# Gate and up products by Strassen's seven products, in a hybrid decoder layer on one core

## The chip, the core and the metric

The kernel runs on one core of a Trainium2 chip. The metric is the device time of one execution in microseconds (us): the median of several runs. One execution was also recorded by the hardware profiler, and every row below is of that execution.

## The reference, cut to what matters

One decoder layer is applied to 1,088 tokens: a prompt of 1,024 and 8 x 8 sample tokens, 1,024 features wide, in 32-bit floats. In order:

- x += 0.5 * (silu(h W_gate) * (h W_up)) W_down, with h = RMSNorm(x); W_gate and W_up are 1,024 x 2,816, W_down is 2,816 x 1,024 (FFN a);
- h = RMSNorm(x), multiplied by w_in (1,024 x 4,096): queries, keys, values, the input u of a state space model (SSM) and two gates; sliding-window attention; the SSM with its own tables of coefficients, followed by a gated linear unit (GLU); the gated sum of both branches times w_out is added to x;
- a second FFN of the same form with weights of its own (FFN b), then a last RMSNorm.

The outputs are y, the key and value windows and the SSM states.

## The kernel before

**Numbers.** Each 32-bit operand of a large product is split in two parts that TensorE multiplies fast: hi, a copy rounded by ScalarE, and lo, the difference from VectorE or GpSimd (`split`, L98). A product then is three: hi·hi, hi·lo, lo·hi (`mm3`, L102). The tokens are on the columns, in three chunks of 384, 384 and 320 (`CH`, L15). x lies in SBUF as 8 tiles of 128 features x 1,088 tokens.

**FFN.** `gu_unit` (L333) makes one tile of 128 of the 2,816 hidden features: per chunk 24 gate products, silu, 24 up products, their product, and its split, which stays in SBUF. `d_unit` (L404) multiplies two or three such tiles by their rows of W_down and adds to x, with VectorE reading PSUM (L432). `ffn_units` (L1467) puts two `gu_unit` before each `d_unit`, so hidden tiles live shortly. The last `d_unit` of FFN a is followed by the next norm, chunk by chunk (`norm_steps`, L291); FFN b ends in `last_unit`, which also makes the output.

**The order of work** is the order in which the program is written out, since the scheduler is in manual mode: every engine and every DMA queue executes its own instructions in that order. `run_units` (L1439) calls for each unit `load` two units ahead (DMAs on SP's queue), `prep` one unit ahead (the splits), and `main`. At each `yield` of a `main`, `tick` (L1420) issues one or more steps of `pending` (norm steps) and, at the rate given, steps of one side job: during FFN a that is `ssm_setup` (L512), started at the first `d_unit` at 0.55 steps per tick. It has 193 steps: the first issues the loads of the parameters, the second transposes `lam` on TensorE, then come small steps with two `pow` on GpSimd (L565, L574), and from step 25 on eight blocks of 21 steps (L673 to L762) that build the tables, almost all of it on VectorE.

**The beginning.** `start_first` (L177) loads three tiles of x, transposes them, and lets the first products of gate and up run on x without the factor of the norm, which is multiplied in afterwards.

**After the mixer**, x is written to DRAM (L936) and reloaded before w_out (`x_reload`, L1386); `wo_unit` (L1391) adds to x and prepares the norm of FFN b.

Of the kernel before, what the change touches and what calls it, by code (L numbers as in the profile page):

```python
# [12 lines left out]
D = 1024  # L13
KC = 8
CH = ((0, 384), (384, 384), (768, 320))  # L15
# [11 lines left out]
# sin x = x (1 + z p(z)), cos x = 1 + z q(z), z = x^2, |x| <= pi/2  # L27
# [4 lines left out]
# columns of the constants: identity, half-swap, block index, sign, parity masks | attention masks, selection  # L32
# [30 lines left out]
class Kern:  # L63
    def __init__(s, ctx, tc, a, o):
# [6 lines left out]
        E(tc.manual_schedule())  # L71
        s.pending = []
# [29 lines left out]
    def mm3(s, ps, ops, every=8):  # L102
        n = 3 * len(ops)
        i = 0
        for wh, wl, xh, xl in ops:
            for w, x in ((wh, xh), (wh, xl), (wl, xh)):
                s.nc.tensor.matmul(ps, w, x, start=i == 0, stop=i == n - 1)  # L107
                i += 1
                if i % every == 0 and i < n:
                    yield  # L110
# [15 lines left out]
    def consts(s):  # L126
# [13 lines left out]
        s.mhalf = s.cst.tile([128, 3], F32, name="mhalf")  # L140
# [3 lines left out]
        s.x = [s.B([128, T], f"x{k}", F32) for k in range(KC)]  # L144

    def htiles(s, ph):
        s.hh = [s.B([128, T], f"hh{k}_{ph}") for k in range(KC)]
        s.hl = [s.B([128, T], f"hl{k}_{ph}") for k in range(KC)]

# [1 line left out]
    def rstd_of(s, c, ms, ph):  # L151
        r = s.small([128, 3], "rstd", 2)
        s.nc.gpsimd.tensor_tensor(r, ms, s.mhalf, op=OP.pow)  # L153
        return r
# [7 lines left out]
    def h_of(s, c, k, rbc, g, eng=None):  # L162
        o, n = CH[c]
        t = s.t(f"hraw{g}_{c}_{k}")
# [3 lines left out]
    def load_x(s, c):  # L168
        nc = s.nc
        for i in range(3 * c, 3 * c + 3):  # L170
# [4 lines left out]
            s.xt.append((t, m))  # L175

    def start_first(s, prep):  # L177
        """the first chunk: h without the factor of the norm, which the first products take instead"""
        nc = s.nc
        V, A = nc.vector, nc.scalar  # L180
        n = CH[0][1]
        g = s.gains[:, 0]
        ssq = s.small([128, 2, 3], "ssq", 2)
        ps = [s.bank(t, f"xtr0_{k}") for k, t in enumerate("aabbmddd")]

        def stats(i):
            t, _ = s.xt[i]
            j1, j2 = s.sm([128, 512], f"junk0_{i}"), s.sm([128, 512], f"junka0_{i}")
            V.scalar_tensor_tensor(j1, t[:, 0:512], 1.0, t[:, 0:512], op0=OP.mult, op1=OP.mult, accum_out=ssq[:, 0, i:i + 1])
            A.activation(j2, t[:, 512:1024], AF.Square, accum_out=ssq[:, 1, i:i + 1])  # L190

        def xc(k):
            if k % 2:
                V.tensor_copy(s.x[k][:, :n], ps[k][:, :n])
            else:
                A.activation(s.x[k][:, :n], ps[k][:, :n], AF.Copy)

        def h(k):
            A.activation(s.hh[k][:, :n], s.x[k][:, :n], AF.Copy, scale=g[:, k:k + 1])
            V.scalar_tensor_tensor(s.hl[k][:, :n], s.x[k][:, :n], g[:, k:k + 1], s.hh[k][:, :n].bitcast(F32), op0=OP.mult, op1=OP.subtract)  # L200

        for i in range(3):
            for k in range(KC):
                nc.tensor.transpose(ps[k][:, i * 128:(i + 1) * 128], s.xt[i][0][:, k * 128:(k + 1) * 128], s.id)
        for i in range(3):
            stats(i)
        ms = s.small([128, 3], "ms", 2)
        V.tensor_add(ms, ssq[:, 0, :], ssq[:, 1, :])
        V.tensor_scalar(ms, ms, 1.0 / D, 1e-6, op0=OP.mult, op1=OP.add)
        rs = s.rstd_of(0, ms, "s")  # L210
        for k in range(0, KC, 2):
            xc(k)
            xc(k + 1)
            h(k)
            if k == 0:
                next(prep)
            h(k + 1)
        next(prep)
        s.hready = 1

        def spread():
            rb = s.spread(0, rs, "s")
            s.rbc0 = s.sm([128, n], "rbc0")
            A.activation(s.rbc0, rb[:, :n], AF.Copy)
        return [spread], [lambda: next(prep)] * 2

    def start_steps(s, c):
        nc = s.nc
        V, A = nc.vector, nc.scalar
        o, n = CH[c]  # L230
        st = {}

        def stats(i, m):
            if "ssq" not in st:
                st["ssq"] = s.small([128, 2, 3], "ssq", 2)
                if n < 384:
                    V.memset(st["ssq"], 0.5)
            t, _ = s.xt[3 * c + i]
            x, y = t[:m, 0:512], t[:m, 512:1024]
            j1, j2 = s.sm([128, 512], f"junk{c}_{i}"), s.sm([128, 512], f"junka{c}_{i}")  # L240
            A.activation(j2[:m], y, AF.Square, accum_out=st["ssq"][:m, 1, i:i + 1])
            V.scalar_tensor_tensor(j1[:m], x, 1.0, x, op0=OP.mult, op1=OP.mult, accum_out=st["ssq"][:m, 0, i:i + 1])

        def rstd():
            ms = s.small([128, 3], "ms", 2)
            V.tensor_add(ms, st["ssq"][:, 0, :], st["ssq"][:, 1, :])
# [1362 lines left out]
```

## Time and profile before

| | |
|---|---|
| median of 3 runs | 2387.35 us (2383.14 to 2388.43) |
| span of the profiled execution, first to last instruction | 2384.7 us |
| TensorE (PE) products, busy | 2349.1 us, 99% of the span |
| VectorE (DVE) busy | 1123.1 us, 47% |
| ScalarE (ACT) busy | 687.7 us, 29% |
| GpSimd (POOL) busy | 169.2 us, 7% |
| DMA | 182.88 MB, 77 GB/s over the span |

No time is given for the profiled execution beyond its span; the span lies 2.65 us under the median of the runs. In the rows, PEld is TensorE's loading of weights, which overlaps its products, and SP is the engine that issues most DMAs. A name such as psga is the PSUM tile of the gate product in FFN a, psdb that of the down product in FFN b. A product's busy time includes its latency; its cost in a stream is the distance from one start to the next.

### The profile page before, as it was taken

What the parts mean: (1) busy time and instruction counts of PE and PEld (TensorE: products, weight loads), DVE (VectorE), ACT (ScalarE), POOL (GpSimd) and SP (SyncE); (2) the same over time, 40 slices, a digit from 0 to 9 for tenths busy, and PEclk for the clock granted to TensorE, in tenths of its full rate; (3) what the DMA queues carried; (4) which work ended last, traced back from release to release, by engine and by line L of the source; (5) the groups of instructions that cost most, each with busy time, mean ns of one, the idle gap of its engine ahead of it and who ended that gap; (6) DMA issues with size and microseconds to landing.
All of it is one profiled execution on the core that took longest, in us unless ns stands there. A gap on an engine that the chain in (4) does not pass through costs nothing. (4 is left out here: it accounts for less than half of the span.)

```text
span 2384.7 us, 34882 instructions
## 1 busy us (share of the span) xinstructions
PE 2349.1 (99%) x14361; PEld 2296.1 (96%) x14361; DVE 1123.1 (47%) x2362; ACT 687.7 (29%) x1483; POOL 169.2 (7%) x241
## 2 busy tenths in 40 slices
PE   8999999999999999999999999999999999999998
PEld 7999999999999997999998999999999999999997
DVE  5655455554432622447773766353332333332324
ACT  5212221222111341246665642231111111111123
POOL 3400000000000130002120200040000000000000
PEclk9999999999999999999999999999999999999999
DMA  5212222222301137631234264101111111111102
GB/s 150 63 47 64 80 63 63 80 64 78 111 27 54 37 144 221 214 93 36 60 83 108 74 227 151 52 27 45 40 50 51 39 53 37 48 41 45 50 22 75
DMA packets 249615, 182.88 MB, mean 77 GB/s; under 512 B 47120, under 2 KB 231504, under 8 KB 249424
## 3 DMA queue, kind: packets, MB, share of 16 engines
q1 hardware_dynamic: 247664, 178.34, 25.4%
q8 instruction: 113, 1.85, 0.3%
q10 hardware_dynamic: 1376, 2.29, 0.3%
q14 instruction: 46, 0.38, 0.0%
q0 software_dynamic: 416, 0.02, 0.0%
HBM read 143.50 MB, written 41.17 MB: 77 GB/s over the span
## 5 line engine op out<-in xcount | busy, mean ns | idle before, releaser
L365 DVE TENSOR_TENSOR sgb<-sgb,psub 128x384 f32<-128x384 f32 (+1 forms) x66 | 35.1, 532 | 270.6 <-PE psub L107 262.7
L432 DVE SCALAR_TENSOR_TENSOR x<-psda,x 128x384 f32<-128x384 f32 (+1 forms) x240 | 125.8, 532 | 68.1 <-PE psda L107 67.5
L432 DVE SCALAR_TENSOR_TENSOR xr<-psdb,xr 128x384 f32<-128x384 f32 (+1 forms) x216 | 114.6, 534 | 83.3 <-PE psdb L107 82.7
L359 ACT ACTIVATE sgb<-psgb 128x384 f32<-128x384 f32 (+1 forms) x66 | 31.3, 474 | 388.2 <-PE psgb L107 388.2
L365 DVE TENSOR_TENSOR sga<-sga,psua 128x384 f32<-128x384 f32 (+1 forms) x66 | 35.0, 530 | 183.9 <-PE psua L107 183.4
L359 ACT ACTIVATE sga<-psga 128x384 f32<-128x384 f32 (+1 forms) x64 | 30.2, 472 | 241.0 <-PE psga L107 241.0
L99 ACT ACTIVATE hidhb<-sgb 128x384 fp32r<-128x384 f32 (+1 forms) x66 | 33.5, 507 | 225.3 <-DVE sgb L365 225.3
L99 ACT ACTIVATE hidha<-sga 128x384 fp32r<-128x384 f32 (+1 forms) x66 | 33.5, 507 | 210.5 <-DVE sga L365 210.5
L1151 POOL TENSOR_SCALAR sm<-sm,sum 128x256 f32<-128x256 f32 x128 | 60.2, 492 | 311.7 <-DVE sum L1149 195.8
L100 POOL TENSOR_TENSOR hl_a<-hraw,hh_a 128x384 fp32r<-128x384 f32 (+1 forms) x72 | 74.5, 1066 | 46.9 <-ACT hh_a L99 42.4
L153 POOL TENSOR_TENSOR rstd<-ms,mhalf 128x3 f32<-128x3 f32 x9 | 8.0, 885 | 927.7 <-DVE ms L304 903.8
L1135 ACT ACTIVATE sm<-sm,nm 128x256 f32<-128x256 f32 x128 | 63.3, 503 | 2.0 <-DVE nm L1122 1.9
L498 POOL TENSOR_TENSOR rf<-msf,mhalf 128x1 f32<-128x1 f32 (+1 forms) x9 | 4.9, 543 | 773.0 <-DVE msf L497 773.0
L100 DVE TENSOR_TENSOR hidla<-sga,hidha 128x384 fp32r<-128x384 f32 (+1 forms) x66 | 35.9, 544 | 38.2 <-ACT hidha L99 38.2
L100 DVE TENSOR_TENSOR hidlb<-sgb,hidhb 128x384 fp32r<-128x384 f32 (+1 forms) x66 | 35.6, 539 | 38.4 <-ACT hidhb L99 38.4
L1118 DVE CUSTOM_DVE_ANT_0 sm<-S,c 128x256 f32<-128x256 f32 x128 | 46.2, 417 | 5.6 <-PE S L1115 5.4
L99 ACT ACTIVATE hh_a<-hraw 128x384 fp32r<-128x384 f32 (+1 forms) x72 | 35.5, 507 | 28.1 <-DVE hraw L165 26.7
L1182 DVE TENSOR_TENSOR ptl<-PT,pth 128x512 fp32r<-128x512 f32 x60 | 38.8, 686 | 3.8 <-ACT pth L1181 3.0
L1204 DVE TENSOR_TENSOR Os<-Os,O 64x256 f32<-64x256 f32 x64 | 26.7, 418 | 26.1 <-ACT Os L1201 25.5
L1181 ACT ACTIVATE pth<-PT 128x512 fp32r<-128x512 f32 x60 | 32.8, 596 | 20.9 <-PE PT L1179 20.6
L1179 PE MATMUL PT<-c,sm 128*128 128x128 f32 x240 | 34.2, 276 | 2.2 <-POOL sm L1151 0.8
L1179 PEld LDWEIGHTS PT<-c,sm 128*128 128x128 f32 x240 | 28.2, 140 | 6.3 <-POOL sm L1151 5.3
(1792 smaller groups left out, 8281.0 us busy)
## 6 DMA issues: line engine op xcount, KB each, us to landing
rgatea<-in_ffn_a_gate_dram SPq DMA_DIRECT2D x22, 512.0 KB, 3.9
rupa<-in_ffn_a_up_dram SPq DMA_DIRECT2D x22, 512.0 KB, 5.2
rdowna<-in_ffn_a_down_dram SPq DMA_DIRECT2D x22, 512.0 KB, 4.5
rgateb<-in_ffn_b_gate_dram SPq DMA_DIRECT2D x22, 512.0 KB, 3.7
rupb<-in_ffn_b_up_dram SPq DMA_DIRECT2D x22, 512.0 KB, 3.9
rdownb<-in_ffn_b_down_dram SPq DMA_DIRECT2D x22, 512.0 KB, 3.5
tab<-tab SPq DMA_DIRECT2D x20, 384.0 KB, 5.9
tab<-tab SPq DMA_DIRECT2D x10, 480.0 KB, 4.9
```

The lines of the kernel that those rows point to most:

```text
L99: s.nc.scalar.activation(hi, raw, AF.Copy)
L100: (eng or s.nc.vector).tensor_sub(lo, raw, hi.bitcast(F32))
L359: nc.scalar.activation(sg[:, :n], pg[:, :n], AF.Silu)
L365: nc.vector.tensor_mul(sg[:, :n], sg[:, :n], pu[:, :n])
L432: nc.vector.scalar_tensor_tensor(xs, ps[:, :n], 0.5, xs, op0=OP.mult, op1=OP.add)
L1118: V.tensor_tensor_reduce(out=sm[:, h, :], in0=ps[:, par * 256:(par + 1) * 256], in1=mask, scale=0.125, scalar=-1e30, op0=OP.add, op1=OP.ma ...
L1135: A.activation(sm[:, h, :], sm[:, h, :], AF.Exp, bias=nm[:, h:h + 1], accum_out=sm4[:, h:h + 1])
L1151: s.nc.gpsimd.tensor_scalar(sm[:, h, :], sm[:, h, :], sm4[:, h:h + 1], 1.0, op0=OP.mult, op1=OP.mult)
L1179: TE.transpose(ps[:, c:c + 128], sm[:, h, kb * 128:(kb + 1) * 128], s.id)
L1181: A.activation(hi, ps, AF.Copy)
L1182: V.tensor_sub(lo, ps, hi.bitcast(F32))
L1204: V.tensor_add(o[r, 0:256], o[r, 0:256], ps[r, c])
```

## The change

- **Gate and up** are seen as one 2 x 2 block product (two halves of the 1,024 input features; gate and up as the two rows) and two groups of tokens as the columns, and are computed by the seven products of Strassen's scheme in place of eight. For this the 1,088 tokens are cut in four quarters of 272: each half of the tokens (`sub`) is a pair of quarters (`e`). Seven operands per half are made from h and split (`hop_steps`: b11, t1 to t4, b21, b22), and seven per tile from the weights (a11, a12, a22, s1 to s4), with four sums on GpSimd (`sums`), seven hi parts on ScalarE and seven lo parts on VectorE, three steps ahead of their use. A unit of the stage is a tile with both halves of the tokens; the first two and the last two tiles are done one half at a time, which makes 26 units. Each product is 12 matmuls of 272 columns. Where Strassen adds products, they accumulate in one PSUM bank across products (X, V).
- The hidden tiles go to DRAM unsplit (`hd`), one DMA per tile and half on SP's queue.
- **Down is a stage of its own** after all of gate and up: eight `d_unit` of 2, 3, 3, 3, 3, 3, 2 and 3 hidden tiles, which load W_down and the hidden tiles and split both; in FFN a the lo parts are made on GpSimd, in FFN b on VectorE. x is written to DRAM before the stage and reloaded in it, four tiles ahead (`need_x`).
- `ssm_setup` still starts with the first `d_unit`, so it now runs in the down stage of FFN a alone, at 1.6 steps per tick.
- The first half of the tokens is normed and all its seven operands are made before the first product (`start`); the second half is made in steps beside the first two units. Before FFN b the same is done in the last `wo_unit` (`normed`).
- GLU and w_out use the four chunks of 272 as well.

The core of the diff:

```diff
-CH = ((0, 384), (384, 384), (768, 320))
+QC = 272
+HC = 2 * QC
+
+CH = {0: (0, 384), 1: (384, 384), 2: (768, 320), 10: (0, QC), 11: (QC, QC), 12: (2 * QC, QC), 13: (3 * QC, QC)}
+CP, CQ = (0, 1, 2), (10, 11, 12, 13)
...
+    def hop_steps(s, sub, R):
+
+        V, P = s.nc.vector, s.nc.gpsimd
+        t = {}
+
+        def sum(n, a, b, into, eng):
+            def f():
+                x = s.B([128, 4, QC], f"{n}raw{sub}", F32) if into is None else R[into]
+                eng.tensor_sub(x, get(a), get(b))
+                t[n] = x
+            return f
+
+        def get(k):
+            return t[k] if k in t else R[k]
+
+        def h(n, k, eng=V):
+            return lambda: s.hsplit(sub, n, get(k), eng)
+        return [h("b11", (0, 0)), sum("t1", (1, 0), (0, 0), None, V), sum("t2", (1, 1), "t1", None, V), h("t2", "t2"), h("t1", "t1"),
+                sum("t3", (1, 1), (1, 0), (1, 0), P), h("b21", (0, 1)), h("t3", "t3"), sum("t4", (0, 1), "t2", (0, 1), P),
+                h("b22", (1, 1)), h("t4", "t4")]
...
+    def normed(s, c):
+
+        sub, e = divmod(c - 10, 2)
+        o = CH[c][0]
+        if e == 0:
+            s.R = s.quarters(sub)
+        R = s.R
+
+        def raw(k, rbc):
+            s.nc.vector.scalar_tensor_tensor(R[e, k // 4][:, k % 4, :], s.x[k][:, o:o + QC], s.gains[:, 2, k:k + 1], rbc[:, :QC], op0=OP.mult, op1=OP.mult)
+        s.pending += s.norm_steps(c, "o", 2, raw)
+        if e:
+            if sub:
+                def spill():
+                    s.x_spill()
+                    s.x = {}
+                s.pending.append(spill)
+            s.pending += s.hop_steps(sub, R)
...
+        for i in range(5):
+            load(i)
+        g.load()
+        for i in range(5, 9):
+            load(i)
+        nc.sync.dma_start(s.c1[:, C_SW:], s.a["c1"][:, C_SW:])
...
+        R = s.quarters(0)
+        for k in range(KC):
+            raw(0, R, k)
+        st = s.hop_steps(0, R)
+        for f in st:
+            f()
+            next(prep, None)
+        for _ in prep:
+            pass
+        for q in range(4):
+            spill(0, q)
...
+        units = [[(j, h)] for h in range(2) for j in range(2)] + [[(j, 0), (j, 1)] for j in range(2, NFF - 2)]
+        units += [[(j, h)] for h in range(2) for j in range(NFF - 2, NFF)]
+        N = len(units)
+        raw, ops, st, hid = {}, {}, {}, {}
+        LEAD = 3
+        steps = []
+        for n in range(N):
+            steps += [("P1", n)] + ([("D", n - 1)] if n else []) + [(k, n) for k in ("P6", "P5", "P27")]
+        steps.append(("D", N - 1))
+        made = {"P1": ("a11",), "D": ("a22", "s4"), "P6": ("s2",), "P5": ("s1",), "P27": ("s3", "a12")}
...
+            g, u = raw[n][:2]
+            if kind == "P6":
+                s1 = s.sm([128, 4, 128], f"s1{ph}{n}")
+                P.tensor_add(s1, u[:, 0:4], u[:, 4:8])
+                P.tensor_sub(u[:, 0:4], g[:, 0:4], u[:, 0:4])
+                P.tensor_sub(g[:, 0:4], s1, g[:, 0:4])
+                raw[n] = g, u, s1
+            if kind == "D":
+                P.tensor_sub(g[:, 4:8], g[:, 4:8], g[:, 0:4])
...
+                    def hi(name=name, n=n2):
+                        w = s.B([128, 2, 4, 128], f"{name}{ph}{n}")
+                        A.activation(w[:, 0], source(name, n), AF.Copy)
+                        ops[n, name] = w
+
+                    def lo(name=name, n=n2):
+                        w = ops[n, name]
+                        V.tensor_sub(w[:, 1], source(name, n), w[:, 0].bitcast(F32))
+                    out += [hi, lo]
+            if i + 1 < len(steps):
+                kind, n = steps[i + 1]
+                if kind in ("P6", "D"):
+                    out.append(lambda: sums(kind, n))
...
+        def prod(ps, n, a, sub, b, more):
+            w = ops[n, a]
+            bh, bl = s.need_op(sub, b)
+            yield from s.mm3(ps[:, :QC], [(w[:, 0, k, :], w[:, 1, k, :], bh[:, k, :], bl[:, k, :]) for k in range(4)], 6, more)
...
+        def p6(n, e):
+            j, sub = units[n][e]
+            d = st[n, e]
+            yield from prod(d["X"], n, "s2", sub, "t2", True)
+            d["u"] = s.t(f"u{ph}{j}_{sub}")[:, :QC]
+            A.activation(d["u"], d["X"][:, :QC], AF.Copy)
...
+        def p3(n, e):
+            j, sub = units[n][e]
+            d = st[n, e]
+            yield from prod(d["V"], n, "s4", sub, "b22", True)
+            V.tensor_add(d["u"], d["u"], d["V"][:, :QC])
+            A.activation(d["u"], d["u"], AF.Silu)
+            P.tensor_mul(d["h2"], d["h2"], d["u"])
+            o = sub * HC
+            nc.sync.dma_start(s.hd[j, :, o:o + HC], hid[j][:, o:o + HC])
...
+                    r = s.B([128, T], f"rhid{ph}{j}", F32)
+                    nc.sync.dma_start(r, s.hd[j])
+                    s.hid[j] = r
 
             def prep(u):
                 st = u.st
+                eng = s.nc.gpsimd if ph == "a" else s.nc.vector
                 for j in js:
-                    s.wsplit(st, j, [128, D], f"dn{ph}{j}")
+                    hi, lo = s.B([128, T], f"hidh{ph}{j}"), s.B([128, T], f"hidl{ph}{j}")
+                    s.split(s.hid[j], hi, lo, eng)
+                    s.hid[j] = hi, lo
+                    yield
...
+                xs = s.need_x(m)[:, o:o + n]
...
+    def need_x(s, k):
+
+        for i in range(min(k + 4, KC)):
+            if i not in s.x:
+                s.x_load(i)
+        return s.x[k]
...
+            free = not getattr(u, "long", False)
+            p = None
+            for step, tok in enumerate(u.main()):
+                free = free or tok == "open"
+                if free:
+                    if p is None:
+                        load(i + 1)
+                        if not any(getattr(v, "long", False) for v in units[i:i + 2]):
+                            load(i + 2)
+                        p = units[i + 1].prep() if i + 1 < N else iter(())
+                    elif step >= 2:
                         next(p, None)
...
+        cuts = (0, 2, 5, 8, 11, 14, 17, 19, 22)
+        out = [s.g_stage(ph)]
+        js = [tuple(range(a, b)) for a, b in zip(cuts, cuts[1:])]
+        out += [s.d_unit(ph, j) for j in js[:-1]]
...
-    at(units[1], before=side(s.ssm_setup, 0.55))
+    at(units[1], before=side(s.ssm_setup, 1.6))
...
```

## Rows read from the trace of the kernel before

**Rows 1.** The page's first part: busy time and instructions of each engine.

```profile
PE 2349.1 (99%) x14361; PEld 2296.1 (96%) x14361; DVE 1123.1 (47%) x2362; ACT 687.7 (29%) x1483; POOL 169.2 (7%) x241
```

**Rows 2.** The chain that ended last, in FFN b: start, length, what.

```profile
1656.02 4.19 PE psgb L107 x24
1660.21 4.16 PE psub L107 x24
...
1679.72 4.19 PE psgb L107 x24
...
1703.42 23.82 PE psdb L107 x144
```

**Rows 3.** Timeline of PE in the attention, products of 256 columns, first and last.

```profile
1050.80 0.28 PE L1114 MATMUL S<-KH,qe 128*128 128x256 f32 x1
...
1051.63 0.28 PE L1115 MATMUL S<-KL,qo 128*128 128x256 f32 x1
1051.75 0.34 PE L107 MATMUL pswga<-hh_a,wga0l 128*128 128x384 f32 x1
```

**Rows 4.** The beginning: busy time by stretch (PE first, all, then xtr alone); timeline.

```profile
0.00:100.00 100.00, 89.33 (x514) 83.29 (x515) 63.14 (x114) 45.02 (x93) 40.59 (x38) 0.97 0.43 116
...
0.00:100.00 100.00, 13.14 (x72) 10.29 (x72) 2.20 (x4) 8.64 (x20) 0.97 0.43 116
...
6.56 0.69 DVE L189 SCALAR_TENSOR_TENSOR junk<-xt 128x512 f32<-128x512 f32 x1 [0.62 <-DMA xt<-in_x_prompt_dram]
...
9.73 0.69 DVE L189 SCALAR_TENSOR_TENSOR junk<-xt 128x512 f32<-128x512 f32 x1 [2.47 <-DMA xt<-in_x_prompt_dram]
...
13.24 0.69 PE L107 MATMUL psga<-hh_a,gatea0h 128*128 128x384 f32 x1 [2.40 <-ACT gatea0h L99]
```

**Rows 5.** Groups by line and shape, VectorE 100 to 620 us, then GpSimd, whole span.

```profile
L432 DVE SCALAR_TENSOR_TENSOR x<-psda,x 128x384 f32<-128x384 f32 x113 | 61.8, 554 | 26.0 <-PE psda L107 25.6
L432 DVE SCALAR_TENSOR_TENSOR x<-psda,x 128x320 f32<-128x320 f32 x57 | 27.8, 488 | 11.3 <-PE psda L107 11.3
L707 DVE TENSOR_TENSOR C<-ae,ssmin 128x576 f32<-128x576 f32 x8 | 6.0, 749 | 0.0
L691 DVE TENSOR_TENSOR S<-ae,ssmin 128x512 f32<-128x512 f32 x8 | 5.5, 684 | 0.0
L747 DVE TENSOR_SCALAR kk<-kk 128x512 f32<-128x512 f32 x8 | 3.4, 427 | 0.3
...
L565 POOL TENSOR_TENSOR prm<-prm 128x32 f32<-128x32 f32 x1 | 5.5, 5462 | 13.6 <-PE psda L107 13.6
L574 POOL TENSOR_TENSOR prm<-prm 128x32 f32<-128x32 f32 x1 | 5.4, 5430 | 6.9 <-DVE prm L571 6.9
```

**Rows 6.** Timeline of VectorE, then of GpSimd, at the norm after FFN a.

```profile
816.54 0.56 DVE L432 SCALAR_TENSOR_TENSOR x<-psda,x 128x384 f32<-128x384 f32 x1 [0.37 <-PE psda L107]
817.02 1.29 DVE L288 TENSOR_TENSOR sqsumf<-sqsumf,sqtf 128x384 f32<-128x384 f32 x1
...
819.23 0.54 DVE L288 TENSOR_TENSOR sqsumf<-sqsumf,sqtf 128x384 f32<-128x384 f32 x1
...
816.88 1.02 POOL L100 TENSOR_TENSOR hl_a<-hraw,hh_a 128x384 fp32r<-128x384 f32 x1 [3.83 <-ACT hh_a L99]
819.53 1.12 POOL L100 TENSOR_TENSOR hl_a<-hraw,hh_a 128x384 fp32r<-128x384 f32 x1 [1.63 <-issue]
```

**Rows 7.** SP's issues of the setup's first step, first and last; then DMA rates (GB/s per 40th) from 13 to 27 us.

```profile
68.73 0.99 SPq L527 DMA_DIRECT2D lam<-in_ssm_lambda_re_dram  x2
...
84.21 3.81 SPq L548 DMA_DIRECT2D kpad<-zero  x8
...
GB/s 332 374 398 421 421 398 410 386 410 456 373 296 345 307 288 287 290 294 290 294 298 372 339 421 398 410 386 410 433 328 138 164 171 158 121 3 0 0 0 0
```

**Rows 8.** Busy time of PE, PEld, DVE, ACT, POOL around the start of FFN b.

```profile
1570.00:1595.00 25.00, 21.72 (x138) 20.88 (x137) 16.02 (x30) 10.97 (x20) 13.00 (x14) 1.00 0.01 2
```

More of the change, by code (lines that the diff above doesn't have):

```diff
@@ L106, in mm3 @@
             for w, x in ((wh, xh), (wh, xl), (wl, xh)):
-                s.nc.tensor.matmul(ps, w, x, start=i == 0, stop=i == n - 1)
+                s.nc.tensor.matmul(ps, w, x, start=i == 0 and not more, stop=i == n - 1, skip_group_check=more)
                 i += 1
@@ L174, in load_x @@
             nc.sync.dma_start(t[:m], src)
[L175 to L184, printed above, removed]
-        def stats(i):
[L187 to L192, printed above, removed]
+            xt[i] = t, m
@@ L272, in sq_add @@
+        s.pending += [bc1, lambda: R1.update(s.quarters(1))]
+        for k in range(KC):
+            if k >= 4:
+                s.pending.append(lambda k=k: tr1(k))
+            s.pending.append(lambda k=k: raw(1, R1, k) if k < 4 else None)
+        s.pending += [lambda k=k: raw(1, R1, k) for k in range(4, KC)]
+        s.pending += [lambda q=q: spill(1, q) for q in range(4)]
+        s.pending += s.hop_steps(1, R1)
     def sq_add(s, c, m, ph):
@@ new lines, in main @@
+            def main(u):
+                s.hop_live = True
+                for i, (kind, n) in enumerate(steps):
+                    if kind == "P1":
+                        load(n + 1)
+                    es = range(len(units[n]))
+                    if kind in ("P1", "P6", "P5"):
+                        parts = [{"P1": p1, "P6": p6, "P5": p5}[kind](n, e) for e in es]
+                    elif kind == "P27":
+                        parts = [p2(n, 0), p7(n, 0)] + ([p7(n, 1), p2(n, 1)] if len(es) > 1 else [])
+                    else:
+                        parts = [f(n, e) for e in es for f in (p4, p3)]
+                    fs = tasks(i + LEAD)
+                    total = 2 * len(parts)
+                    done = 0
+                    for p in parts:
+                        for _ in p:
+                            done += 1
+                            while fs and len(fs) > (total - done) * 2:
+                                fs.pop(0)()
+                            if fs:
+                                fs.pop(0)()
+                            yield "open" if n >= N - 1 else None
+                    for f in fs:
+                        f()
+                s.hop = {}
@@ L1415, in main @@
                     if last:
-                        s.pending += s.norm_steps(c, *last)
+                        last(c)
         return U()
@@ L1560, in body @@
     units += [s.wo_unit((m,)) for m in range(5)]
[L1562 to L1564 removed]
+    units.append(s.wo_unit((5, 6, 7), s.normed))
     units += s.ffn_units("b", None)
[L1566 to L1578 removed]
+    s.start(units[0])
+    s.run_units(units)
     s.flush()
```

376 lines of the change are left out of this document (195 added, 181 removed).

## The prediction, written before the change was run

> **What bounds the kernel now.** I read the page's engine shares first, then the chain that ended last, then the timeline for what one product costs, and only then the side engines. PE is busy 99% and VectorE 47% [rows 1]; the chain in an FFN is nothing but products, 24 for a chunk of gate and 24 for one of up [rows 2]. Busy time counts latency, so I go by distances: two hidden tiles start 1679.72 - 1656.02 = 23.70 us apart, which are 144 products. A group of 24 with 384 columns takes 4.16 us, 0.173 each; the other 48, with 320 columns, share 23.70 - 4 x 4.16 = 7.06 us, 0.147 each. So every product beside a product is paid for, and hardly anything else is: the kernel is product-bound, and a change gains by columns taken away and loses by whatever makes PE wait.
>
> **1. Seven products for eight: -111 us.** A tile takes 7 products x 2 halves x 12 = 168 matmuls of 272 columns, against 144 wider ones. The nearest width in the trace is 256: eight of these take 1051.75 - 1050.80 = 0.95 us, 0.119 each [rows 3]. Between that and 0.147 at 320, 272 columns come to 0.126. 168 x 0.126 = 21.17 us, 2.53 less than 23.70, for 44 tiles 111 us. Bounds: 107 at 0.1265, 115 at 0.1255.
>
> The weights' load of each product is hidden in these rows. [...]
>
> **2. GLU and w_out in four chunks: +4 us.** Eight units of each, 24 products per chunk: 24 x 4 x 0.126 = 12.10 against 24 x (2 x 0.173 + 0.147) = 11.84, 0.26 more, sixteen times.
>
> **3. The beginning: +22 us.** Before, the first 100 us hold 514 products, of which 72 transpose x and about a dozen others are small [rows 4]; some 430 at 0.165 are 71 us, so 29 us went to things other than FFN products. After, five tiles of x must have landed, not three (statistics of the third at 9.73, of the second at 6.56: the fifth at about 11). VectorE then does statistics and copies (about 5 us), 16 gain products of 272 columns (0.45 each, 7), and the split of b11 and a11 (1.2 + 0.6): first product near 25, against 13.24. For the other operands it has ten more steps of 1,088 columns at 1.2 and six weight parts at 0.6, and two sums of GpSimd of 2.6 that hold it (part 5): the operand of the fourth product is ready near 43, when 4.5 us of products are done. The second half of the tokens is 42 pending steps, some 35 us of VectorE beside the 18 us of products that need nothing of it: 12 more. That makes about 39 + 12 = 51 us not spent on products, 22 more than 29. Bounds: 12 if the second half is hidden, 32 if GpSimd's sums hold VectorE each time.
>
> In the steady part of the stage I charge nothing. Per tile of 21.2 us VectorE has 7 lo parts (0.65) and 8 PSUM reads (0.4), 8 us; ScalarE about as much; GpSimd four sums (1.3) and two products (0.75), 7 us; all is issued three steps, at least 9 us, ahead. If that cover were gone, each tile would wait for its lo parts.
>
> **4. The first down unit of FFN a: +30 us.** This is where the change adds a wait. SP must pass the last hidden tile's store, which waits for GpSimd's product, so the reload of x starts some 2.5 us after the stage. At its first tick the unit issues, in this order, four tiles of x (2.2 MB), the loads of the next two down units (6.5 MB), and then the setup's first step, `lam` foremost. The setup's second step, one tick later, transposes `lam` on PE, and behind it on PE stand all the unit's other products. 8.7 MB at about 380 GB/s (290 to 420 in rows 7) take 23 us: `lam` is there some 27 us after the stage, and PE has had 4 us of products. GpSimd's queue comes next: the `pow` that waits for the same load (5.5 us), six lo parts for the second unit (2.6 each: 1.02 for 384 columns [rows 6], scaled to 1,024 and 1,088 less a fixed part) and the second `pow` (5.4) [rows 5]. They end 26 us after `lam`, at 53; the second unit should have started at 23.7 (144 products at 0.165). Bounds: 20, where only `lam` is waited for at the full 420 GB/s, and 33. The 29 DMAs of that step also occupy SP for 19 us [rows 7], and x tiles 4 to 7 stand behind them; they land inside the wait.
>
> **5. Down units two to four of FFN a: +60 us.** The setup's 168 table steps at 1.6 per tick last 105 ticks; a unit of three tiles has 36 ticks and 216 products, 35.5 us, so the stretch is 104 us of products. VectorE's share of one block is 12 x 0.684 + 3 x 0.749 + 5 x 0.427 + 0.4 = 13.0 us [rows 5]; following instructions overlap by 0.08 (816.54 + 0.56 against 817.02 in rows 6), which leaves about 12.1. Eight blocks are 97; the 70 readings of PSUM in the stretch at 0.53 - 0.08 are 32. 129 us of VectorE beside 104 of products: 25 us over, and as VectorE frees PSUM in order, PE pays them. Before, the same work lay in 530 us.
>
> To this comes GpSimd. At 817.02 an addition of two SBUF tiles on VectorE took 1.29 us in place of 0.54 (819.23) while GpSimd, from 816.88, ran a subtraction of 1.02; the reading of PSUM (L432) keeps its 0.56 [rows 6]. Nearly all table steps have two SBUF inputs. The three units hold 18 lo parts of GpSimd of 2.6 us, 47 us in all; VectorE is on PSUM or one-input steps for about a quarter of it, so 35 us are lost. Bounds: 25 without any of this, 68 with the 47 nearly in full.
>
> [...]
>
> **6. FFN b: +14 us.** The operands of the first half are made under the last chunks of w_out (18 us for some 25 us of VectorE), but the second half's reach into the third unit: 6 us over the 25 - 21.72 = 3 us idle that stand there now [rows 8]. In the first down unit, x waits 2.5 us for the last store and tile 4 of x stands behind 8.7 MB: it lands 28 us after the stage, wanted at 19: 8 us. Bounds 5 and 25.
>
> **7. The rest: +4 us.** After waits as long as in 4 some products run at a lower granted clock (0.97 on average over the first 100 us in rows 4), and single-half units have little room. W_down's products are the same in number; the splits moved with them are hidden in FFN b, where VectorE has 20 us per 35.5.
>
> **Sum:** -111 + 4 + 22 + 30 + 60 + 14 + 4 = +23. The profiled execution has a span of 2384.7 us, and the median of the runs is 2.65 above it; I add 23 to the median: **2410 us**. What a measurement of this kernel can tell from no change is about 0.2%, 5 us.
>
> **Rivals.**
> - *GpSimd does not hold VectorE (faster).* The place is units two to four, with the chain in unit one. For it: the 0.54 at 819.23, with GpSimd starting at 819.53 [rows 6], shows that meeting is not the rule; against it: the 1.29. Then 35 go in part 5, 8 in part 4 (only `lam` is waited for) and 5 in part 3: 2410 - 48 = 2362. It decides when less than about 20 of these 48 remain. Chance 0.37.
> - *The stage of gate and up is bound by its operands.* VectorE, ScalarE, GpSimd and PE pass every sum on in a ring; if each tile waited 1.5 us for one, 44 x 1.5 = 66: 2476. Against it: 8 us of work per 21, issued 9 us ahead. Chance 0.08.
> - *Products of 272 columns are no cheaper.* If each had a fixed cost such that a tile stays at 23.7, 111 are not gained: 2521. The straight line through 256, 320 and 384 columns speaks against it. Chance 0.03.
>
> **How the numbers follow.** The forecast has the remaining 0.52; its own range is 2390 to 2450, parts 4 and 5 within their bounds. The whole range runs from the low ends together (-115 + 4 + 12 + 20 + 25 + 5 = -49: 2338) to the high ends of the larger parts (2452), which leaves out the last two rivals and some of the first. Faster by over 0.2% is the first rival and a little of the forecast's low side: 0.38. Within 0.2%: 0.08. Slower: 0.54.
>
> **What would show it.** Right: 272-column products 0.126 us apart and tiles 21.2 apart in mid-stage; the first Strassen product near 25 us; PE idle about 20 us early in the first down unit, ended by the load of `lam`; VectorE above 95% busy through units two to four with additions of over 1 us among them, and PE following it; no waits after the setup ends. Wrong: units two to four at 35.5 us each, or a stage of gate and up with tiles over 22 us apart.

## The result and the profile after

The changed kernel takes **2537.0 us** (median of 4 runs, 2533.8 to 2539.3) against 2385.5 of the kernel before on the same chip: a ratio of 1.063 (95% interval 1.061 to 1.064), some 151 us slower. The forecast was 23 us slower. The sign was right, the size was not.

The page's first part answers to [rows 1]; the second line is the granted clock in 40 slices of the span.

```profile
PE 2304.0 (91%) x15810; PEld 2238.7 (88%) x15810; DVE 1410.1 (56%) x2733; ACT 883.5 (35%) x1973; POOL 647.4 (26%) x541
...
PEclk7899999997888999999999999996999999989999
```

PE is busy 91% in place of 99%, and GpSimd 647 us in place of 169. A slice is 63 us: the clock is low at the beginning (slices 1 and 2), in the setup's stretch (10 to 13) and where FFN b's gate and up starts and ends (28 and 36).

The stages can be settled from single products. The timeline of PE shows, in FFN a, the first product of all, of the fourth tile, of the first of the last two (single-half) tiles, of the down stage and of the mixer; then the fourth tile, the last two and the down stage of FFN b:

```profile
23.41 0.60 PE L113 MATMUL Xa<-b11h,a11a 128*128 128x272 f32 x1 [7.18 <-ACT b11h L104]
...
134.95 0.29 PE L113 MATMUL Xa<-b11h,a11a 128*128 128x272 f32 x1
...
495.13 0.29 PE L113 MATMUL Xa<-b11h,a11a 128*128 128x272 f32 x1
...
562.89 0.34 PE L113 MATMUL psda<-hidha,dna0h 128*128 128x384 f32 x1
...
962.36 0.34 PE L113 MATMUL psu<-hh,wu0h 128*128 128x384 f32 x1
...
1726.18 0.43 PE L113 MATMUL Xb<-b11h,a11b 128*128 128x272 f32 x1
...
1815.27 0.29 PE L113 MATMUL Xb<-b11h,a11b 128*128 128x272 f32 x1
...
2175.44 0.29 PE L113 MATMUL Xb<-b11h,a11b 128*128 128x272 f32 x1
...
2243.03 0.34 PE L113 MATMUL psdb<-hidhb,dnb0h 128*128 128x384 f32 x1
```

In the kernel before, the first products of the mixer and of FFN b are these:

```profile
832.50 0.34 PE L107 MATMUL psu<-hh_a,wu0h 128*128 128x384 f32 x1
...
1582.12 0.34 PE L107 MATMUL psgb<-hh_a,gateb0h 128*128 128x384 f32 x1
```

- **Steady stage:** 134.95 to 495.13 is 17 tiles at 21.19 us from the start of one to that of the next (their pitch), with no wait at all; 1815.27 to 2175.44 in FFN b gives the same.
- **Beginning:** a tile's first product stands ahead of the last 4 of the 14 products of the tile before it. Up to 134.95 PE has done 3 - 4/14 tiles, 57.5 us; 77.4 us went elsewhere, 48 more than the 29 before.
- **End of FFN a's gate and up:** 495.13 to 562.89 is 67.8 us for 2 + 4/14 tiles, 48.4: 19 lost.
- **Down in FFN a:** 399.5 us for 22 x 72 products at (2 x 0.173 + 0.147) / 3 = 0.164, 260, and 17 us of small products (the setup's and the norm's, 15 of which FFN a had before too): 122 lost. 51 of them lie ahead of the first step of the setup's first block (645.3 us), where 82.4 us hold 31 of down products.
- **FFN b:** 89.1 - 57.5 = 31.6 at the start, 67.6 - 48.4 = 19 at the end of gate and up.
- **By whole stages:** FFN a ends 129.9 us later than before (962.36 against 832.50), the mixer with w_out takes 14.2 more (763.8 against 749.6), FFN b with the output 7.3 more: 151. In the mixer, w_out takes 111.9 us in place of 99.5, and only 1.3 of that are its products.

Who made PE wait, the longest first (waits of the whole span: us in total, times, longest):

```profile
PE vl L893 <- DVE S L888: 62.9, 8, 15.0
PE lamT L745 <- DMA lam<-in_ssm_lambda_re_dram: 23.1, 1, 23.1
PE Xb L113 <- DVE hidb L523: 14.6, 7, 3.4
PE Xa L113 <- ACT hida L491: 14.6, 1, 14.6
PE Xa L113 <- DVE hida L523: 12.8, 6, 3.8
...
PE rbco L160 <- POOL rstd L154: 8.4, 2, 7.9
```

The setup's transposes (`vl`) come first, and the wait for `lam` stands where the forecast had it: 23.1 us, early in the first down unit. Busy time by stretch, in the columns of [rows 8] (PE, its weight loads, VectorE, ScalarE, GpSimd; the last three are the granted clock, the DMA engines' share and GB/s): the beginning, the steady stage, the wait for `lam`, the rest of the setup in two parts, and the down stage behind it.

```profile
23.00:100.00 77.00, 47.80 (x275) 42.53 (x276) 65.29 (x85) 33.99 (x60) 36.86 (x20) 0.73 0.35 111
150.00:530.00 380.00, 375.09 (x2962) 374.65 (x2962) 179.09 (x273) 136.00 (x306) 140.77 (x109) 1.00 0.26 78
563.00:592.00 29.00, 5.74 (x31) 5.26 (x30) 2.81 (x8) 6.60 (x7) 2.35 (x4) 0.62 0.82 314
592.00:630.00 38.00, 27.31 (x147) 25.29 (x147) 33.10 (x77) 2.40 (x4) 29.76 (x10) 0.95 0.46 157
630.00:840.00 210.00, 146.12 (x804) 137.66 (x804) 168.58 (x288) 47.09 (x69) 47.61 (x18) 0.85 0.33 96
840.00:930.00 90.00, 90.00 (x545) 90.00 (x544) 37.02 (x68) 12.65 (x14) 34.28 (x15) 1.00 0.29 96
```

VectorE is the busiest engine of the beginning (65 of 77 us) and of the setup (169 of 210), yet in the setup it is idle a fifth of the time, and PE three tenths. The forecast's own sign, VectorE above 95% busy through these units, did not come.

### The profile page after: what moved, and what is told of

Read it like the earlier page. It is cut to its first block, busy times and chain, and to the rows that moved or that the text cites. A ratio compares the mean times of both kernels' runs of the same rounds, so it can differ in the third digit from the quotient of the medians.

```text
span 2536.1 us, 39996 instructions
## 1 busy us (share of the span) xinstructions
PE 2304.0 (91%) x15810; PEld 2238.7 (88%) x15810; DVE 1410.1 (56%) x2733; ACT 883.5 (35%) x1973; POOL 647.4 (26%) x541
## 5 line engine op out<-in xcount | busy, mean ns | idle before, releaser
L625 DVE SCALAR_TENSOR_TENSOR xr<-psda,xr 128x384 f32<-128x384 f32 (+1 forms) x192 | 100.8, 531 | 89.4 <-PE psda L113 82.7
L625 DVE SCALAR_TENSOR_TENSOR xr<-psdb,xr 128x384 f32<-128x384 f32 x168 | 87.3, 532 | 104.2 <-PE psdb L113 90.8
L113 PE MATMUL Xb<-t4h,a22b 128*128 128x272 f32 x352 | 80.2, 307 | 14.6 <-DVE hidb L523 14.6
L113 PE MATMUL Xa<-t4h,a22a 128*128 128x272 f32 x352 | 77.0, 298 | 12.8 <-DVE hida L523 12.8
L113 PE MATMUL Xa<-t2h,s2a 128*128 128x272 f32 x352 | 72.3, 294 | 14.6 <-ACT hida L491 14.6
L113 PE MATMUL Yb<-b21h,a12b 128*128 128x272 f32 x352 | 76.6, 297 | 9.0 <-DVE a12b L466 6.5
L113 PE MATMUL Xa<-b11h,a11a 128*128 128x272 f32 x352 | 73.8, 298 | 9.2 <-ACT b11h L104 8.7
L113 PE MATMUL Xa<-t3h,s3a 128*128 128x272 f32 x352 | 73.8, 297 | 6.5 <-ACT ua L499 6.5
L113 PE MATMUL Vb<-b22h,s4b 128*128 128x272 f32 x352 | 77.6, 300 | 0.0
L113 PE MATMUL Ya<-b21h,a12a 128*128 128x272 f32 x352 | 75.3, 293 | 0.9 <-DVE a12a L466 0.7
L113 PE MATMUL Va<-b22h,s4a 128*128 128x272 f32 x352 | 74.7, 292 | 0.0
L113 PEld LDWEIGHTS Xa<-t4h,a22a 128*128 128x128 f32 x352 | 60.1, 195 | 14.2 <-DVE hida L523 14.2
```

Source lines behind the costliest of these rows:

```text
L113: s.nc.tensor.matmul(ps, w, x, start=i == 0 and not more, stop=i == n - 1, skip_group_check=more)
L625: nc.vector.scalar_tensor_tensor(xs, ps[:, :n], 0.5, xs, op0=OP.mult, op1=OP.add)
```

## The experiments

Two theories stood at the start. **Theory 1:** GpSimd's two-input instructions, which hold VectorE and are slow links between engines, cost most of what exceeds the forecast. **Theory 2:** the setup, packed at 1.6 steps per tick, is simply more than VectorE can do beside the down stage. What speaks for the first is the timeline of VectorE and of GpSimd in the setup:

```profile
630.83 0.19 DVE L848 TENSOR_TENSOR ae<-pw 128x32 f32<-128x32 f32 x1
631.06 2.54 DVE L849 TENSOR_TENSOR pw<-ae 128x32 f32<-128x32 f32 x1
633.52 2.37 DVE L850 TENSOR_TENSOR pw<-ae 128x32 f32<-128x32 f32 x1
635.93 2.40 DVE L851 TENSOR_TENSOR ae<-pw 128x32 f32<-128x32 f32 x1
...
631.01 2.53 POOL L105 TENSOR_TENSOR hidla<-rhida,hidha 128x1088 fp32r<-128x1088 f32 x1 [5.02 <-ACT hidha L104]
633.51 2.33 POOL L105 TENSOR_TENSOR dna6l<-rdowna,dna6h 128x1024 fp32r<-128x1024 f32 x1
635.81 2.46 POOL L105 TENSOR_TENSOR hidla<-rhida,hidha 128x1088 fp32r<-128x1088 f32 x1
```

Three steps of a form that takes 0.19 us just ahead of them (630.83) last as long as the lo part beside each: 2.54, 2.37 and 2.40 us beside 2.53, 2.33 and 2.46. How often the two engines meet decides what that costs.

**Lo parts on VectorE.**

```diff
-                eng = s.nc.gpsimd if ph == "a" else s.nc.vector
+                eng = s.nc.vector
```

> Only the lo parts of the activations in FFN a's down stage go to VectorE instead of GpSimd (48 subtractions of 128x272 or 256, some 0.44 us each there, 21 us in all). Theory 1 (GpSimd holds VectorE: the 128x32 steps of the setup took 2.3 to 2.5 us beside lo parts of the same length, against 0.18 us): the stretch of the setup, which costs 96 us now, loses about half of that, and the kernel takes about 2487 us. Theory 2 (the setup at 1.6 steps per tick is simply more VectorE work than the stretch has): VectorE gets 21 us more to do, and the kernel takes about 2558 us. Unchanged within 10 us would speak for neither.

Measured: 2521.2 us, 16 less. Neither. The expectation had the size wrong: there are 44 of these subtractions, of 128 x 1,088 or 1,024 elements, which took 113.5 us on GpSimd and take 55.0 us here, not 21. Taken with the run without lo parts below (39.5 us less), they cost 24 us on VectorE.

**The setup slower.** `side(s.ssm_setup, 0.95)` in place of 1.6.

> Only the rate of the state-space setup beside FFN a's down stage is changed, from 1.6 to 0.95 steps per tick. Theory 2 (too much VectorE work in the stretch): it fits then, the 96 us of the stretch vanish, about 2441 us. Theory 1 (GpSimd holds VectorE): the lo parts still hold it, at each tick fewer of the setup's steps are met; a gain of some 40 us, about 2497 us, with waits left at the same transposes.

Measured: 2509.9, 27 less, which is short of both. The wait at `vl` falls from 62.9 to 16.1 us, but 23.3 us at the PSUM that VectorE frees, and 7.4 at the products `k`, take its place.

**`lam` later.** 24 yields in place of one ahead of its transposes.

> Only the point is moved at which TensorE takes up the transposes of lam: 24 steps of the setup's order later, so that the load of lam, which lands 23 us after TensorE asks for it, has landed. If that wait is on the path by itself, both theories give about 20 us less, 2517 us. The rival: the wait for lam hides other work that is late too (the lo parts of the first unit, the reload of x), and the next wait takes its place: 2532 us.

Measured: 2539.8, no gain: the rival was right. PE stands still as long, 23.66 us, at a PSUM tile that VectorE has to read, and VectorE waits for the fifth tile of x, which is queued behind the same loads as `lam` (timeline of VectorE):

```profile
607.51 2.39 DVE L625 SCALAR_TENSOR_TENSOR xr<-psda,xr 128x384 f32<-128x384 f32 x5 [27.61 <-DMA xr<-xd]
```

**The gate and up stage without GpSimd.** In `hop_steps` and `g_stage`:

```diff
-        V, P = s.nc.vector, s.nc.gpsimd
+        V, P = s.nc.vector, s.nc.vector
...
-        V, A, P = nc.vector, nc.scalar, nc.gpsimd
+        V, A, P = nc.vector, nc.scalar, nc.vector
```

> In the gate and up stages alone, all sums of the Strassen operands, the product of GLU halves and the temporaries that GpSimd had go to VectorE, so that GpSimd does nothing there. Theory 1 (GpSimd's slow two-input steps are links of the operand chain, and hold VectorE): the beginning gets 15 us shorter, the ends of the two stages 15 each, the beginning of FFN b 10: about 2482 us. The rival (VectorE is then overloaded in the steady part, where it would have about 15 of each 21 us to do): no change or 10 us more, 2537 to 2547 us.

Measured: 2509.9, 27 less, half of what theory 1 gave. Gate and up take 527 us in place of 540 in FFN a and 502 in place of 517 in FFN b. What those links were is to be read at the end of FFN b's stage, in single-half units (PE, VectorE, ScalarE and GpSimd of the changed kernel):

```profile
2193.20 0.39 PE L113 MATMUL Xb<-t4h,a22b 128*128 128x272 f32 x1 [2.46 <-DVE hidb L523]
...
2192.11 0.69 DVE L466 TENSOR_TENSOR s2b<-rgateb,s2b 128x512 fp32r<-128x512 f32 x1 [2.85 <-ACT s2b L461]
2192.72 0.43 DVE L523 TENSOR_TENSOR hidb<-hidb,Xb 128x272 f32<-128x272 f32 x1
...
2191.45 0.63 ACT L461 ACTIVATE s2b<-rgateb 128x512 fp32r<-128x512 f32 x1 [4.12 <-POOL rgateb L444]
...
2190.14 1.27 POOL L444 TENSOR_TENSOR rgateb<-s1b,rgateb 128x512 f32<-128x512 f32 x1
```

PE waits for a reading of PSUM that needs nothing but PE's own product; but on VectorE it stands behind the lo part of s2, that behind ScalarE's hi part, and that behind the fourth of GpSimd's sums in a row. Without these links the stages' ends are 5.6 (FFN a) and 9.2 us (FFN b) shorter and the starts 6.8 and 6.0, though VectorE is busy 70 of the 77 us from 23 to 100 in place of 65. The wait at the second product of all stays as it was, 14.6 us.

**No lo parts at all** (the hi part twice, in FFN a's down stage).

> Leaves out part of the computation: in FFN a's down stage no lo parts are made, the hi part stands in their place in the products, which are the same in number. It takes the lo parts away from GpSimd without giving them to VectorE. What the stretch of the setup still loses of its 96 us is then due to the setup alone. Theory 1 (GpSimd holds VectorE): 25 to 35 us are left, the kernel takes about 2472 us. Theory 2 (the setup at this rate is more than VectorE and the chain of small transposes can pass on): 65 to 75 us are left, about 2512 us.

Measured: 2497.5, 39.5 less, between the two. How long the setup's blocks take (from the first step of one to that of the next) is read from the first and last of the eight; VectorE's step that begins a block, in the changed kernel, then in this run (after the colon stand the durations in ns, then the first and the last start in us):

```profile
L884 DVE TENSOR_TENSOR S<-ae,ssmin x8: 681/682/686, 645.3 to 813.8; 128x512 f32<-128x512 f32 x8
```

```profile
L894 DVE TENSOR_TENSOR S<-ae,ssmin x8: 680/682/684, 618.8 to 774.0; 128x512 f32<-128x512 f32 x8
```

A block now takes (774.0 - 618.8) / 7 = 22.2 us; in the changed kernel (813.8 - 645.3) / 7 = 24.1. At 1.6 steps per tick a block has 13.0 us of down products. So GpSimd costs 1.9 of the 11.1 us that a block loses, though in these seven blocks VectorE is busy 134.5 us with GpSimd's lo parts and 112.4 without: of 22 us of holding, 13 lengthen the stretch. The rest of the 39.5 us lies ahead of the blocks, where the stage of gate and up ends 9.6 us earlier (in the changed kernel four lo parts, from 542.1 to 553.1, stand in GpSimd's queue ahead of that stage's last sum) and the first down unit and the setup's first steps are 17 shorter. The run takes away the holding and the products' waits for late lo parts together; it does not part the two.

**Transposes later in the order.** Six yields more ahead of `vl` and of `k` in each block, at 2.4 steps per tick.

> The changed kernel, with one thing moved: in each block of the setup the transposes of S (vl) and the small products of C and S (k) stand six steps further behind the VectorE work that they wait for, at 2.4 steps per tick in place of 1.6, so that the setup ends where it did (289 steps for 193). Without any lo parts the stretch still lost some 72 us in which VectorE was busy 73% only. If that is a hand-over (TensorE stands at vl for VectorE, and then VectorE stands for TensorE's products), most of the 8 waits of 3.6 to 15 us at vl go and the kernel gains 30 to 50 us: about 2495 us. If it is VectorE's amount of work, the waits move to the reading of PSUM and the gain is under 10 us: about 2530 us.

Measured: 2537.3, nothing gained; a block takes 24.2 us as before. What moved is only where PE waits (43.8 us at `vl`, 20.2 at PSUM).

**Without the setup's own products, with and without lo parts.** The four transposes and four products of a block are left out, ScalarE copies their sources:

```diff
-            pv = s.bank("m", f"vl{q}")
-            for g in range(4):
-                nc.tensor.transpose(pv[:, g * 128:(g + 1) * 128], S[:, g].rearrange("p s c -> p (s c)"), s.id)
...
-            A.activation(vl, pv.rearrange("p (g x) -> p g x", g=4), AF.Copy)
+            A.activation(vl, S.rearrange("p g s c -> p g (s c)"), AF.Copy)
...
```

> Leaves out the lo parts of FFN a's down stage, as the run without lo parts did (2497.5 us), and also the setup's own products on TensorE in its eight blocks (transposes vl and products k; ScalarE copies S and C themselves in their place), so that TensorE meets the setup only through the PSUM tiles that VectorE reads. The products' own time, about 2.1 us a block, 17 in all, goes in any case. Turns (TensorE stands at vl for VectorE and VectorE then stands for TensorE's products, 44 us of waits of VectorE in that stretch): the 72 us still lost fall to the 25 by which VectorE has too much work, about 2440 us. Amount (VectorE's work alone sets the pace): 17 us less only, 2480 us.

> As the run before it, but with the lo parts on GpSimd as in the changed kernel: only the setup's products on TensorE in its blocks are left out. Beside 17 us for the products' own time: if turns cost 40 to 45 us here too, about 2477 us, and GpSimd's lo parts then cost what is left over the run before it, some 35 to 40 us. Amount: 2520 us.

Measured: 2472.6 and 2512.2, each 24.8 or 24.9 below its partner with the products. The products' own time, from the start of one to that of the next, is 13 us in the changed kernel (the expectations had 17), so standing for each other in turns costs 12, not 40. The pair differs by 39.6, GpSimd's share again. Without lo parts and products a block still takes (754.2 - 620.5) / 7 = 19.1 us:

```profile
L894 DVE TENSOR_TENSOR S<-ae,ssmin x8: 682/683/687, 620.5 to 754.2; 128x512 f32<-128x512 f32 x8
```

Why is in VectorE's timeline of that run:

```profile
672.65 0.43 DVE L943 TENSOR_SCALAR kc<-kk 128x512 f32<-128x512 f32 x1 [6.24 <-DMA kpad<-ks]
...
678.43 0.69 DVE L894 TENSOR_TENSOR S<-ae,ssmin 128x512 f32<-128x512 f32 x1
...
695.22 0.43 DVE L956 TENSOR_SCALAR kk<-kk 128x512 f32<-128x512 f32 x1 [0.90 <-ACT kk L953]
696.02 0.68 DVE L894 TENSOR_TENSOR S<-ae,ssmin 128x512 f32<-128x512 f32 x1
```

From 678.43 to 696.02 VectorE is hardly idle but for ScalarE's answers: 17.6 us for one block with its readings of PSUM, 16.3 of them busy. Two waits for a store to leave a buffer that the next table wants (6.2 and 7.0 us) are 1.9 a block more on average. Of the 24.1 us of the changed kernel, then, 19.1 are VectorE's chain and its waits for buffers, 1.6 the small products, 1.5 turns and 1.9 GpSimd.

**The beginning with less for VectorE.** The lo parts of the second half's operands are left out.

> The changed kernel with one part of the computation left out: the lo parts of the seven operands of the second half of the tokens in FFN a (the hi part stands in their place), 7 x 1.28 = 9 us of VectorE's work in the first 100 us. If VectorE's work sets the pace of the beginning, 8 to 9 us less, about 2528 us. If it is the links by GpSimd and ScalarE or the order, 0 to 3 us less.

Measured: 2530.4 (2527.1 to 2533.7), 6.6 less. The fourth tile of gate and up starts 7.7 us earlier, at 127.30. That speaks for VectorE's work as the pace of the beginning; two other runs speak against its amount alone (with the sums on VectorE above, and the last run below).

**Towards a better version.** First the setup is put into FFN a's gate and up, where VectorE has half its time free (179 of 380 us):

```diff
                     if kind == "P1":
                         load(n + 1)
+                        if ph == "a" and n == 5:
+                            s.side, s.rate, s.acc = s.ssm_setup(), 0.45, 0.0
```

> Only the place of the state-space setup is changed: it starts with the sixth unit of FFN a's gate and up at 0.45 steps per tick, so that the down stage is alone with its own work; the transposes of lam stand eight steps behind its load. Down in FFN a took 400 us and should take about what FFN b's takes, 240 plus some 25 for its longer last unit: 135 us less. The gate and up stage gets some 10 us of the setup's own small products and, where VectorE still has room (190 of 400 us busy there), nothing more: about 2417 us. The rival (GpSimd's sums hold the setup's steps there just as the lo parts did in the down stage, so that the lo parts of the weights come late): some 60 us of it come back, about 2475 us.

Measured: 2450.5, 86.5 less, between the two. Down in FFN a takes 279 us, 121 less; gate and up 575 in place of 540, 13 of it the setup's small products; VectorE is busy 305 of the 380 us.

> As the run with the setup in the gate and up stage, and with all sums of the operands, the last product of the GLU halves and the lo parts of FFN a's down stage on VectorE, so that GpSimd has nothing in the FFNs but pow. If GpSimd's holding of VectorE costs more than its work is worth, the gain of 27 us measured for the sums alone comes on top: about 2390 us. The rival: VectorE, with some 330 of 400 us busy in the gate and up stage, is late with lo parts: 2420 us or more.

Measured: 2408.7, 42 less, between the two: with more instructions VectorE is busy 295 of 380, less than before. Here what GpSimd held back was worth more than what it did. All of the gain lies in the stages of gate and up, 29 us in FFN a and 15 in FFN b; down in FFN a stays at 279, so once the setup is gone from it, it makes no difference which engine makes the lo parts.

> As the run before it, and at the beginning only the split of b11 is made ahead of the first product; the other operands of the first half are made when a product first needs them. The wait of 14.9 us at the second product, where the reading of the first product's PSUM stands behind the split of t4 on ScalarE, should fall to some 5 us: 10 us less than the run before it, about 2380 us. The rival: VectorE's work on the operands sets the pace there, whatever the order: the wait moves to the third and fourth products, 0 to 3 us less.

Measured: 2410.9, no gain: the wait at the second product falls from 14.6 to 6.2 us, and waits at later ones take its place. Next, x ahead of the last stores (`need_x(0)` at product P5 of the last unit, `need_x(4)` between the loads of the next two units):

> As the run with the setup in the gate and up stage and all of GpSimd's sums on VectorE, and the reload of x starts ahead of the last two stores of hidden tiles on SP's queue, its second four tiles ahead of the loads of the down unit after next. The waits of the two first down units for x (10 and 12 us, with some clock behind them) go: about 2390 us. The rival: SP's queue then waits for memory to come free, and the last stores come later: no gain.

Measured: **2379.5**, ratio 0.9966 to the kernel before (0.9953 to 0.9979), which is less than either expectation and 8 us less than the kernel before. Down takes 265 us in FFN a and 226 in FFN b, 14 less each. What x had waited for is SP's queue; first in the changed kernel, then in this run:

```profile
553.87 11.31 SPq L541 DMA_DIRECT2D hd<-hida  x2
565.28 1.83 SPq L1594 DMA_DIRECT2D xr<-xd  x4
```

```profile
560.54 1.83 SPq L1599 DMA_DIRECT2D xr<-xd  x4
572.67 0.32 SPq L541 DMA_DIRECT2D hd<-hida  x1
```

> As the run before it, and the last unit of w_out has four tiles in place of three, so that the operands of FFN b's gate and up have 48 us of products over them in place of 36. The waits around the start of FFN b (10.9 us at the norm's broadcast, 7.4 at the operands, some 39 us in all with w_out's end) lose about 12: about 2378 us. The rival: the norm's broadcast waits for VectorE at a fixed place of the order, whatever the cover: 0 to 3 us less.

Measured: 2375.6, ratio 0.995 (0.9935 to 0.9965); its interval overlaps that of the run before it. The wait at the broadcast goes, but one of 9.2 us at VectorE's sum of squares comes.

> As the run before it, and at the beginning ScalarE, which is busy 34 of the 77 us there, takes the statistics of the last four tiles of x and the copies of the second half from VectorE, which is busy 65 to 70 of them: 5 us of VectorE's work. If VectorE sets the pace of the beginning, 4 to 5 us less: about 2374 us. If it is the order of the operands, nothing.

Measured: 2375.6, ratio 0.996 (0.994 to 0.998): nothing. VectorE is busy 64.8 of the 77 us from 23 to 100 in place of 69.3, and the fourth tile starts at 130.84 in place of 130.62; by the expectation's own terms that speaks for the order of the operands. The best version stands at 2376, 12 us under the kernel before.

## Why the prediction was wrong

| part | forecast | measured |
|---|---|---|
| 1 products, 44 x (23.70 - 21.19) | -111 | -110 |
| 2 GLU (96.2 us, before 94.9) and w_out in four chunks | +4 | about +3 |
| 3 beginning | +22 | +48 |
| end of FFN a's gate and up | in 7 | +19 |
| 4 and 5 first down unit and setup | +90 | +122 |
| 6 FFN b: start 31.6 - 3 and 11 at w_out's end, end of stage 19, down 14 | +14 | +73 |
| what FFN a lost before outside its beginning, and other small terms | | -4 |
| sum | +23 | +151 |

128 us were missed: 100 at the seams, the places where one stage ends and the next begins (parts 3, 6 and 7: 26 at the beginning, 15 at the end of FFN a's gate and up, 59 around FFN b), 21 in part 4 and 11 in part 5. (The high bounds of the parts add up to 2446, not to the range's 2452.)

**Right:** part 1 to two hundredths (21.17 forecast, 21.19 measured), and with it the straight line through 256, 320 and 384 columns. The weights' loads overlap running products here, too: in the steady stage the products start 0.126 us apart, and one load lasts 0.19 us. The steady stage was charged nothing and cost nothing. The wait for `lam` came as forecast, 23 us, and that x's second half lands in the same time is shown by the run with `lam` moved. GpSimd's share by its lo parts in FFN a was right in sum, 35 and 8 forecast, 39.5 and 39.6 measured by two pairs; that is luck, since its place was not (15 and 17 where the forecast had 35 and 8, and 9.6 ahead of the stage, where it had nothing).

**Wrong, parts 4 and 5.** "Eight blocks are 97 ... 25 us over": the step that failed took VectorE's own instructions, 12.1 us of tables and 4 of readings per block, as all that a block needs. As work that was right, 16.3 busy in the block shown. But a block takes 17.6 with ScalarE's answers, 19.1 on average with the waits for buffers, and with the small products and turns 22.2 without GpSimd, against 13.0 of down products: 9.2 x 8 = 73 us, or 60 without the small products' own time (13), in place of 25. GpSimd's 35 in these blocks were 15. The two errors nearly cancel, so that part 5 is off by 11 only. Part 4 had 30 and lost 51: the 23 for `lam` came, the lo parts cost 17 in place of 8, and some 11 no run parts further.

**Wrong, part 3.** First product at 23.41 (25 forecast), but the operands of the first half and the second half cost 26 us more than the 13.5 and 12 reckoned. The sum of VectorE's work was there, only its cover was not: a single-half unit needs new weight operands all the same, and those stand in VectorE's queue between the second half's steps. VectorE is busy 65 of 77 us, and taking 9 us of work from it gave 7.7. But the amount of its work does not settle it: with GpSimd's sums added to it the fourth tile started 6.5 us earlier (128.47), and with 4.5 us of it on ScalarE nothing was gained. So the links through GpSimd are 6.5 of the 26; how the rest is shared between VectorE's work and the order of the queues stays open. Made in another order, the operands moved the waits and gained nothing.

**Wrong, parts 6 and 7,** the largest share. "Single-half units have little room" had 4 us for everything. Each end of gate and up cost 19 us, from the chain POOL, ACT, DVE, PE shown above (5.6 and 9.2 of them went with GpSimd's sums) and, in FFN a, from the lo parts of the first down unit (9.6); the rest is not shown by a run. Around FFN b's start part 6 had the first half's operands hidden under w_out and 6 us for the second half's. The chain that ended last shows what came of it, at w_out's end:

```profile
1705.99 0.35 DVE sqsumo L363
1706.34 1.21 DVE t1raw L186
...
1720.08 1.20 DVE t4l L105
...
1723.37 0.90 PE rbco L160 x3
```

The norm of the second half (`sqsumo`, then the broadcast `rbco` on PE) stands in VectorE's queue behind the first half's operands, and PE waits 7.9 us for it; FFN b's start then loses 31.6 us in the way of the beginning, 6.0 of them by GpSimd's sums. The 14 us of the down stage, for 8, are the wait for x: they went when x was loaded ahead.

The first rival (GpSimd does not hold VectorE) falls by the rows of 631 to 636 and by the 22 us of holding in the seven blocks. The second, a gate and up stage bound by its operands, is what the steady stage excludes and the stage's two ends show.

## What to carry over

A product-bound kernel is lengthened by its seams: a stage that is free in the middle lost 19 to 77 us at each end here, where the units are half as long, the next stage's preparation comes in and each in-order queue joins them. Cost a seam by the chain that its operands pass from engine to engine, in the order of each queue, against the products that need nothing of it; the work of the busiest side engine alone does not give it (the beginning became 6.5 us shorter while VectorE got more to do). And cost side work packed beside products by the distance from one block of it to the next, with its waits for answers and buffers, not by the sum of its instructions. Here it paid to give GpSimd no two-input work where VectorE is on the path: with the setup in gate and up it gave 42 us to take it away, and 27 with the setup elsewhere, although VectorE then had more to do.

## What the runs showed of the hardware

After a wait of 14 us PE's products ran at about half their pace for 3 us, at a granted clock of 0.50. The stretches are the last 14 us before the transposes at 720, the 3.3 us behind them and the 6 us after that, in the columns of [rows 8]; then two products of 384 columns in the second stretch:

```profile
706.00:720.00 14.00, 0.00 (x0) 0.01 (x1) 12.29 (x17) 3.98 (x6) 5.03 (x3) 0.64 0.20 50
720.10:723.40 3.30, 3.30 (x12) 3.30 (x13) 1.92 (x3) 0.60 (x1) 1.99 (x1) 0.50 0.22 63
724.00:730.00 6.00, 5.76 (x38) 5.24 (x37) 4.10 (x9) 0.59 (x1) 0.00 (x0) 1.00 0.22 59
...
721.22 0.52 PE L113 MATMUL psda<-hidha,dna5h 128*128 128x384 f32 x1
721.54 0.52 PE L113 MATMUL psda<-hidla,dna5h 128*128 128x384 f32 x1
```

They start 0.32 us apart in place of 0.173. The forecast had 4 us for this and the single-half units together. In the whole run the granted clock is at 0.5 for 235 us, in which PE is busy 124.5, against 21 and 14.9 in the kernel before (sums of the stretches at 0.5). At a granted clock of 1.00 these products would take half the time, as 0.173 stands to 0.32, so by this estimate the clock is at most 62 - 7 = 55 of the 128 us missed. It is no part beside the others but lies inside the seams and the blocks, and how much of it PE would have spent waiting for operands anyhow no run shows.

GpSimd's hold shows in the means of single lines, too: of the setup's steps of 128 x 512 elements, 0.68 us in [rows 5], the two dearest lines of the stretch take 1.2 us on average (groups of VectorE, 592 to 840), and in the run without lo parts 0.68 both:

```profile
L934 DVE TENSOR_TENSOR lo<-c,prm 128x512 f32<-128x512 f32 x8 | 9.8, 1219 | 0.0
L922 DVE TENSOR_TENSOR W<-ae,ssmin 128x512 f32<-128x512 f32 x8 | 9.7, 1208 | 0.0
```
